# The lo half of every second weight part made by an adding DMA, in the output projection and gate of a bidirectional encoder layer

## The chip, the cores and the metric

The kernel runs on one core of a Trainium2 chip. The metric is the device time of one execution in microseconds; less is better. Profiles come from the hardware profiler, one execution each. Engines are named as in the profile: PE (matrix multiply; PEld loads its weights), DVE (vector engine), ACT (scalar engine), POOL (GpSimd), SP (the engine that issues most DMAs). Instructions that only issue a DMA are not counted as busy; an issuing queue is written with a q (SPq).

## The reference

One encoder layer over 256 tokens of width 2048, in float32:

```python
hn = _rmsnorm(h, norm_w[i])
proj = hn @ w_in[i]                                   # 2048 x 18432
q, v, f_fwd, f_bwd, z_a, b_gate, c_gate, h_b, z_b = jnp.split(proj, IN_SPLITS, axis=-1)
o_a = _hgrn2_bidirectional(jax.nn.silu(q), v, f_fwd, f_bwd, lb_all[:, i])
o_a = _head_rmsnorm(o_a, hgrn_norm_w[i]) * jax.nn.silu(z_a)
y_b = b_gate * _short_conv(c_gate * h_b, conv_w[i])
o_b = _rmsnorm(y_b, conv_norm_w[i]) * jax.nn.silu(z_b)
h = h + jnp.concatenate([o_a, o_b], axis=-1) @ w_out[i]   # 4096 x 2048
gate = jax.nn.sigmoid(h @ w_ple_gate[i])                  # 2048 x 2048
h = h + (p[i] @ w_ple[i]) * gate                          # 256 x 2048
return _rmsnorm(h, final_norm_w)
```

The change concerns the weights of the two products `@ w_out` and `@ w_ple_gate`.

## The kernel before

**Two halves for each number.** Each factor is kept as hi, the number cast to float32r, and lo, the number minus hi, also in float32r. A product is then hi x hi + hi x lo + lo x hi. In the output projection and the gate these are three matmuls, L636 (hi of the activations, hi of the weights), L637 (hi, lo) and L638 (lo, hi).

**The stream of weights.** All weights pass through the class `Stream`. `add` puts a block of the weights of up to 1 MB on the list `todo` and cuts it into parts of 128 x 1024 numbers (512 KB); a part has a number, its place in `where`. `load` issues the DMA of one block from SP's queue (L57) into a tile `raw` (3 buffers). `split` makes hi with a cast on ACT (L70) and lo with a subtraction on DVE (L71), in one tile `spl` (5 buffers) in which hi and lo rows alternate. `get(i)` returns part i and first opens all parts up to i + 3 (`ahead` is 3). Splits are emitted at a raised priority (`high_priority(offset=300)`). The order of the instructions on each engine comes from the tile framework's scheduler, by priority and readiness; only the first blocks of the kernel are ordered by hand.

**The stages.** (1) The input projection: 72 blocks of columns, `gemm_in`, L289 and L290, with the recurrence of group A and the convolution of group B worked in between. (2) The output projection: four blocks j of 512 columns, each with 8 blocks of 1 MB from `w_out`; `gemm_tok` runs over 32 row tiles, first those of group A into `pa`, then those of group B into `pb`, for both halves m of the tokens. A part of 128 x 1024 holds two row tiles of 512 columns, so PE runs 12 matmuls on it. After each j the residual `hh` is updated on DVE (L657, L661) and transposed for the next product (L646 on PE, L649 on ACT, L650 on DVE). (3) The gate: columns of 512, 512, 512, 256 and 256 (`GCOLS`); ahead of each 512 columns stands the product with `w_ple` (`pp`, one part, copied to `pl` in L722). In the two columns of 256 a part holds four row tiles. `gated` makes the sigmoid on ACT (L683), multiplies and adds on DVE (L686, L687), squares on ACT (L694) and multiplies by the final norm's weight on POOL (L695). The last column runs its four parts twice, first for m = 0, then for m = 1, each followed by `finish(m)`, which scales and stores.

At the border between (1) and (2) the last group of B is still being worked: POOL L314 and L587, ACT L580, L594 and L608, and the loads of `hh` (2 MB, L618) and `pr` (L622).

Of the kernel before, what the change touches and what calls it, by code (L numbers as in the profile page):

```python
# [11 lines left out]
AF = mybir.ActivationFunctionType  # L12
ALU = mybir.AluOpType
# [17 lines left out]
class Stream:  # L31


    def __init__(self, tc, rawp, splp, ahead):
        self.tc, self.nc, self.rawp, self.splp, self.ahead = tc, tc.nc, rawp, splp, ahead
        self.todo = []
        self.where = []
        self.raws = {}
        self.parts = {}
        self.next = 0  # L40

    def add(self, src):

        j = len(self.todo)
        _, k, n = src.shape
        self.todo.append((src, k, n))
        first = len(self.where)
        self.where += [(j, h) for h in range(k * n // 1024)]
        return list(range(first, len(self.where)))
# [9 lines left out]
    def open(self, i):  # L59
# [6 lines left out]
        self.parts[i] = part.rearrange("p (k s n) -> p k s n", s=2, n=n)  # L66
        return half, self.parts[i]

    def split(self, r, v):
        self.nc.scalar.copy(out=v[:, :, 0, :], in_=r)  # L70
        self.nc.vector.tensor_tensor(out=v[:, :, 1, :], in0=r, in1=v[:, :, 0, :], op=ALU.subtract)  # L71

    def get(self, i):
        while self.next <= min(i + self.ahead, len(self.where) - 1):
            if self.next not in self.parts:
                part = self.open(self.next)

                with self.tc.high_priority(offset=300):
                    self.split(*part)
            self.next += 1  # L80
        return self.parts[i]

# [2 lines left out]
def tile_hymba_encoder(  # L85
# [31 lines left out]
    ws = Stream(tc, rawp, splp, 3)  # L117
# [8 lines left out]
    oblocks = [sum((ws.add(w_out[j, h]) for h in range(8)), []) for j in range(4)]  # L126
    gblocks, pblocks = [], []
    for j, (c0, n) in enumerate(GCOLS):
        if c0 % 512 == 0:
            pblocks.append(ws.add(w_ple[c0 // 512]))  # L130
        if n == 512:
            gblocks.append(sum((ws.add(w_gate[j, h]) for h in range(4)), []))
        else:
            gblocks.append(sum((ws.add(w_gate_end[j - 3, h]) for h in range(2)), []))


    few = const.tile([P, 16], F32, name="few")
# [43 lines left out]
    for j in range(4):  # L181
        sgn = 1 if j < 2 else -1
        pool.affine_select(
            out=tri[:, j, :], in_=tri[:, j, :], compare_op=ALU.is_ge, fill=0.0, base=0,
# [369 lines left out]
    for i in range(8):  # L554
# [9 lines left out]
        for m in range(2):  # L564
            ct = 2 * i + m
            dve.tensor_scalar(cg[:, m, :], u[:, m, 0:T], cvw[:, 0, ct : ct + 1], None, op0=ALU.mult)
            for j in (1, 2):
                dve.scalar_tensor_tensor(
                    out=cg[:, m, :], in0=u[:, m, j : j + T], scalar=cvw[:, j, ct : ct + 1],
# [11 lines left out]
        for m in range(2):  # L581
            ct = 2 * i + m
            dve.scalar_tensor_tensor(
                out=hb[:, m, :], in0=hb[:, m, :], scalar=cnw[:, ct : ct + 1], in1=sz[:, m, :],
# [67 lines left out]
    for j in range(4):  # L652
# [7 lines left out]
        for m in range(2):  # L660
            dve.scalar_tensor_tensor(  # L661
                out=hh[:, m, cs], in0=pb[m], scalar=rb[:, m : m + 1], in1=hh[:, m, cs], op0=ALU.mult, op1=ALU.add
# [128 lines left out]
```

## Time and profile before

| | |
|---|---|
| runs | 1145.67, 1146.47, 1147.21 us; median 1146.47 |
| profiled execution, own time | 1148.26 us |
| its span in the profile | 1146.5 us |
| granted PE clock, mean | 0.994 |
| DMA, whole span | 214.31 MB, mean 187 GB/s |
| stage of the output projection and the gate | 860.65 to 1137.90 us of the span |

The profiled execution's own time is that of the execution that the profiler recorded; its span is the stretch from the first to the last instruction in it. In a line of a group, the columns are: line, engine and operation, tiles written and read, shapes, count, busy time and mean ns of one, and the idle time of the engine just before them with what ended it. In a timeline a line is start, duration, engine, line, operation; in brackets is the idle time before it and what ended it.

### The profile page before, as it was taken

Reading aid. Unit: us, or ns where it says so; the run is one execution under the profiler, and the core shown is the slowest. Engines: PE = TensorE matmul, PEld = TensorE weight load, DVE = VectorE, ACT = ScalarE, POOL = GpSimd, SP = SyncE. Lnnn points to the kernel's source line nnn. Section 1 sums busy time; section 2 is a strip of 40 time slices with the busy share of each in tenths; the row PEclk is TensorE's granted clock in tenths of the full one; section 3 lists DMA queues with packets and bytes.
Section 4 is the critical chain, followed back from the end, with each engine's and each line's share of the span. In section 5 each row is a group of like instructions: output and inputs, shape, how many; then the busy total and the mean of one; then the engine's idle time right before and its main releaser. Section 6 shows DMA issues by size and latency. Waiting matters only on the chain.

```text
span 1146.5 us, 16966 instructions
## 1 busy us (share of the span) xinstructions
PE 1130.4 (99%) x6832; PEld 980.6 (86%) x6832; DVE 739.8 (65%) x954; ACT 644.4 (56%) x896; POOL 210.9 (18%) x167
## 2 busy tenths in 40 slices
PE   8989999999999999999999999999999999999997
PEld 7878888888888888888888888888888888888886
DVE  7695859585858686775566566566656555555664
ACT  6676667585858585765544444444545434434554
POOL 1031414140413223232121211211211000000011
PEclk9999999999999999999999999999999999999999
DMA  9653545455455545464555555555557555565542
GB/s 317 261 196 111 189 156 190 165 182 177 156 185 177 170 169 184 152 214 153 188 197 198 185 184 188 187 198 182 201 184 266 187 198 192 194 216 188 202 166 75
DMA packets 32911, 214.31 MB, mean 187 GB/s; under 512 B 3648, under 2 KB 5056, under 8 KB 8512
## 3 DMA queue, kind: packets, MB, share of 16 engines
q1 hardware_dynamic: 32688, 213.14, 54.1%
q8 instruction: 54, 0.88, 0.3%
q14 instruction: 25, 0.20, 0.0%
q10 hardware_dynamic: 144, 0.08, 0.0%
HBM read 211.11 MB, written 2.10 MB: 186 GB/s over the span
## 4 chain that ended last, share of the span: by engine, by line
PE 97%; DMA 1%; ACT 1%; POOL 0%; DVE 0%; SPq 0%; issue 0%; ACTq 0%
PE a L289 46%; PE a L290 23%; PE pg L637 3%; PE pg L636 3%; PE pg L638 3%; PE pa L636 3%; PE pa L638 3%; PE pa L637 3%; PE pb L636 3%; PE pb L637 3%; PE pb L638 3%; PE scps L466 1%; PE cx L508 1%; PE o L518 1%; DMA xf<-in_xt_dram 1%; PE o L519 1%
## 5 line engine op out<-in xcount | busy, mean ns | idle before, releaser
L71 DVE TENSOR_TENSOR spl<-raw,spl 128x1024 fp32r<-128x1024 f32 (+2 forms) x394 | 503.7, 1281 | 324.9 <-ACT spl L70 324.4
L289 PE MATMUL a<-xs,spl 128*128 128x512 f32 x1792 | 632.0, 397 | 1.2 <-ACT spl L70 1.2
L70 ACT CAST spl<-raw 128x1024 fp32r<-128x1024 f32 (+2 forms) x394 | 406.6, 1035 | 354.9 <-PE a L290 219.3
L290 PE MATMUL a<-xs,spl 128*128 128x256 f32 x1792 | 501.5, 280 | 1.1 <-DVE spl L71 1.0
L289 PEld LDWEIGHTS a<-xs,spl 128*128 128x128 f32 x1792 | 337.4, 188 | 77.5 <-ACT spl L70 2.1
L290 PEld LDWEIGHTS a<-xs,spl 128*128 128x128 f32 x1792 | 338.9, 189 | 2.4 <-DVE spl L71 2.3
L289 PE MATMUL a<-spl,xs 128*128 128x512 f32 x512 | 178.6, 393 | 0.0
L290 PE MATMUL a<-spl,xs 128*128 128x256 f32 x512 | 143.6, 281 | 0.0
L289 PEld LDWEIGHTS a<-spl,xs 128*128 128x128 f32 x512 | 95.9, 187 | 21.4
L290 PEld LDWEIGHTS a<-spl,xs 128*128 128x128 f32 x512 | 96.9, 189 | 0.0
L309 ACT COPY r<-a 128x256 f32<-128x256 f32 x112 | 41.0, 368 | 45.1 <-PE a L290 45.0
L695 POOL TENSOR_TENSOR hh<-hh,fw 128x512 f32<-128x512 f32 (+1 forms) x10 | 11.5, 1152 | 259.2 <-ACT gt L694 249.7
L636 PE MATMUL pg<-spl,ht 128*128 128x512 f32 (+1 forms) x160 | 55.7, 348 | 0.0
L638 PE MATMUL pg<-spl,ht 128*128 128x512 f32 (+1 forms) x160 | 55.5, 347 | 0.0
L637 PE MATMUL pg<-spl,ht 128*128 128x512 f32 (+1 forms) x160 | 55.5, 347 | 0.0
L636 PE MATMUL pa<-spl,mixa 128*128 128x512 f32 x128 | 50.5, 394 | 0.0
L638 PE MATMUL pa<-spl,mixa 128*128 128x512 f32 x128 | 49.9, 390 | 0.0
L637 PE MATMUL pa<-spl,mixa 128*128 128x512 f32 x128 | 49.9, 390 | 0.0
L637 PE MATMUL pb<-spl,mixb 128*128 128x512 f32 x128 | 49.8, 389 | 0.0
L636 PE MATMUL pb<-spl,mixb 128*128 128x512 f32 x128 | 49.8, 389 | 0.0
L638 PE MATMUL pb<-spl,mixb 128*128 128x512 f32 x128 | 49.8, 389 | 0.0
L504 POOL TENSOR_TENSOR s<-scm 128x256 f32<-128x256 f32 x16 | 17.9, 1121 | 113.1 <-DVE scm L502 113.1
(166 smaller groups left out, 1093.5 us busy)
## 6 DMA issues: line engine op xcount, KB each, us to landing
raw<-in_w_in_dram SPq DMA_DIRECT2D x138, 1024.0 KB, 5.0
raw<-in_w_out_dram SPq DMA_DIRECT2D x32, 1024.0 KB, 5.0
raw<-in_w_gate_dram SPq DMA_DIRECT2D x12, 1024.0 KB, 5.0
raw<-in_w_in_dram SPq DMA_DIRECT2D x9, 512.0 KB, 10.2
raw<-in_w_gate_end_dram SPq DMA_DIRECT2D x4, 1024.0 KB, 4.9
xf<-in_xtok_dram SPq DMA_DIRECT2D x2, 1024.0 KB, 12.6
hh<-in_xtok_dram SPq DMA_DIRECT2D x1, 2048.0 KB, 7.9
raw<-in_w_ple_dram SPq DMA_DIRECT2D x4, 512.0 KB, 3.6
```

The lines of the kernel that those rows point to most:

```text
L70: self.nc.scalar.copy(out=v[:, :, 0, :], in_=r)
L71: self.nc.vector.tensor_tensor(out=v[:, :, 1, :], in0=r, in1=v[:, :, 0, :], op=ALU.subtract)
L289: pe.matmul(a, lhsT=lh, rhs=rf, start=(kt == 0), stop=False)
L290: pe.matmul(a[:, :T], lhsT=ll, rhs=rh, start=False, stop=(kt == NKT - 1))
L309: act.copy(out=r, in_=acc[m][:, 1, :])
L466: pe.matmul(scps[s0 : s0 + Q, 2 * d + hf, t0 : t0 + w], lhsT=lhsT, rhs=rhs, start=True, stop=True)
L504: pool.tensor_tensor(out=s, in0=sm[:, 0:2, :], in1=sm[:, 2:4, :], op=ALU.add)
L508: pe.matmul(cx[:, d, :], lhsT=kx[:, d, h, :], rhs=qc[:, d, h, :], start=True, stop=True)
L636: pe.matmul(acc[m], lhsT=lh, rhs=w[:, k, 0, :], start=(kt == 0), stop=False)
L637: pe.matmul(acc[m], lhsT=lh, rhs=w[:, k, 1, :], start=False, stop=False)
L638: pe.matmul(acc[m], lhsT=ll, rhs=w[:, k, 0, :], start=False, stop=(kt == nk - 1))
L695: pool.tensor_tensor(out=h, in0=h, in1=fw[:, cs], op=ALU.mult)
```

## The change

Every second part of the output projection's and the gate's weights (`late[1::2]`, 48 of 96 parts; always the second half of a block of 1 MB) is split in another way. ACT makes hi with the same cast as before and then writes -hi to the place of lo. A DMA issued from POOL's queue then reads the same 512 KB of weights from HBM once more and adds them to -hi in SBUF, so that lo stands there when it has landed. The DVE subtraction of these parts is gone. The product with `w_ple` and the whole input projection are split as before.

```diff
@@ class Stream
+        self.by_dma = ()
...
+    def split_by_dma(self, i, r, v):
+
+        j, h = self.where[i]
+        src, k, n = self.todo[j]
+        kp = 1024 // n
+        self.nc.scalar.copy(out=v[:, :, 0, :], in_=r)
+        self.nc.scalar.activation(v[:, :, 1, :], r, AF.Copy, scale=-1.0)
+        self.nc.gpsimd.dma_start(v[:, :, 1, :], src[:, kp * h : kp * h + kp], accum_op=ALU.add)
+
     def split(self, r, v):
...
                 with self.tc.high_priority(offset=300):
-                    self.split(*part)
+                    if self.next in self.by_dma:
+                        self.split_by_dma(self.next, *part)
+                    else:
+                        self.split(*part)
...
+    late = sum(oblocks, []) + sum((g for g in gblocks), [])
+    ws.by_dma = set(late[1::2])
```

## The prediction

> **What bounds the kernel now.** I read the page first (engine shares and the chain), then the busy time in the stage that the change touches, then the waits in it, and last the instructions of one part in order of time.
>
> ```profile
> span 1146.5 us, 16966 instructions
> PE 1130.4 (99%) x6832; PEld 980.6 (86%) x6832; DVE 739.8 (65%) x954; ACT 644.4 (56%) x896; POOL 210.9 (18%) x167
> PE 97%; DMA 1%; ACT 1%; POOL 0%; DVE 0%; SPq 0%; issue 0%; ACTq 0%
> ```
>
> PE is 99% busy and the chain of work that ended last is PE for 97% of the span. An average can hide a stage, so here is the stage of the output projection and the gate alone, from its first matmul to its last:
>
> ```profile
> core 0: us, PE busy (x) PEld busy (x) DVE busy (x) ACT busy (x) POOL busy (x), PEclk, DMA share, GB/s
> 860.65:1137.90 277.25, 277.21 (x1328) 233.39 (x1328) 153.41 (x155) 125.49 (x149) 14.34 (x11) 1.00 0.54 189
> ```
>
> PE is busy for 277.21 of 277.25 us at full granted clock. DVE, which loses work by the change, has 124 us to spare there. The waits in this stretch (engine, line, whom it waited for, total, times, longest) say who sets the pace:
>
> ```profile
> POOL hh L695 <- ACT gt L694: 249.7, 7, 195.6
> DVE spl L71 <- ACT spl L70: 117.1, 92, 1.7
> ACT spl L70 <- PE pb L638: 53.4, 32, 1.7
> ACT spl L70 <- PE pa L638: 42.5, 28, 1.7
> ACT spl L70 <- PE pg L638: 32.6, 20, 1.8
> ```
>
> No row has PE waiting. The splits wait for PE: ACT's cast of a part (hi, L70) waits until PE releases one of the five `spl` buffers. So faster splitting has nothing to give, and what matters is whether a split can become late.
>
> **The cover.** ACT in order of time, in the gate:
>
> ```profile
> 1052.31 1.05 ACT L70 CAST spl<-raw 128x1024 fp32r<-128x1024 f32 x1 [1.67 <-PE pg L638]
> 1055.03 1.05 ACT L70 CAST spl<-raw 128x1024 fp32r<-128x1024 f32 x1 [1.67 <-PE pg L638]
> ```
>
> One part takes PE 1055.03 - 1052.31 = 2.72 us. With five buffers the cast of part k starts when PE ends part k-5; PE then works on k-4 to k-1. The second half of a split therefore has 4 x 2.72 = 10.88 us from the start of the cast before PE asks for it. The wait of 1.67 us in front of each cast also shows that ACT has room for one more instruction of 1.05 us per pair of parts.
>
> **The change part by part.** The instructions of a split today (minimum/median/maximum in ns), in that stage:
>
> ```profile
> L70 ACT CAST spl<-raw x96: 1034/1050/1057, 859.9 to 1123.6; 128x1024 fp32r<-128x1024 f32 x96
> L71 DVE TENSOR_TENSOR spl<-raw,spl x96: 1216/1226/1636, 861.0 to 1124.6; 128x1024 fp32r<-128x1024 f32 x96
> L57 SPq DMA_DIRECT2D raw<-in_w_out_dram x27: 327/328/328, 865.9 to 1010.2; - x27
> ```
>
> Of 96 parts, `late[1::2]` takes 48, each time the second part of a 1 MB load. *Removed*: 48 x 1.226 = 59 us of DVE, off the path, worth nothing, since nothing waits for DVE there but the lo matmuls, which are covered. *Added on ACT*: an ACTIVATE with scale -1. The nearest rows are 128x512, the cast and the activations:
>
> ```profile
> L694 ACT ACTIVATE gt<-hh 128x512 f32<-128x512 f32 x6 | 3.8, 629 | 2.0 <-DVE hh L687 2.0
> L649 ACT CAST ht<-ht 128x512 fp32r<-128x512 f32 x8 | 4.7, 584 | 2.4 <-PE ht L646 2.4
> ```
>
> The two cost the same within 0.05 us, so at 128x1024 I take the cast's 1.05 us. It fits in the 1.67 us gap; -hi is there 2 x 1.05 = 2.10 us after the cast began. Four times, at the edges between gate columns, ACT is packed with L683, L694 and L722 and the extra 1.05 us pushes later casts: between 0 and 4.2 us in all, and I take 1.0, near the lower end, because gaps of 1.67 us follow each edge and give the time back.
>
> *Added on POOL*: the DMA is issued there and waits there for -hi. No POOL DMA is in this trace. Below is SP's 0.33 us (L57 above), above a POOL instruction on a tile:
>
> ```profile
> L587 POOL TENSOR_TENSOR cg<-cg,hb 128x512 f32<-128x512 f32 x1 | 2.3, 2292 | 3.6 <-DVE hb L583 3.6
> L314 POOL TENSOR_TENSOR hb<-hb,rbc 128x512 f32<-128x512 f32 x1 | 1.3, 1292 | 7.6 <-DVE hb L310 7.6
> ```
>
> I take 1.3 us. POOL is otherwise idle for almost 200 us on end, so nothing queues behind these waits in the output projection; L695 does in the gate, and nobody waits for L695 until the last lines.
>
> *Added on the DMA engines*: 48 x 0.5 MB, read a second time from HBM and added to what stands in SBUF. The trace has no adding DMA. Issues by line, with the time from issue to landing:
>
> ```profile
> raw<-in_w_ple_dram SPq DMA_DIRECT2D x4, 512.0 KB, 3.6
> raw<-in_w_out_dram SPq DMA_DIRECT2D x32, 1024.0 KB, 5.0
> hh<-in_xtok_dram SPq DMA_DIRECT2D x1, 2048.0 KB, 7.9
> xf<-in_xtok_dram SPq DMA_DIRECT2D x2, 1024.0 KB, 12.6
> DMA to landing us min/median/max: 4.8/5.0/9.6
> ```
>
> (The last line is for the raw loads from 866 to 960 us.) The lower end is a plain 512 KB, 3.6 us. The upper end is 12.6 us, a load in the saturated start. In between: the raw buffer's last reader is now the -1 activation, so SP issues the next 1 MB load just when the adding DMA starts, and both use the same engines; if the sum counts twice (source and destination are read), 2 MB are on their way together, and 2 MB took 7.9 us. That is the row it is nearest to, and I take 7.9.
>
> So lo lands 2.10 + 1.3 + 7.9 = 11.3 us after the cast began (6.0 at the lower end, 2.10 + 2.3 + 12.6 = 17.0 at the upper), against a cover of 10.88: late by 0.4 us. Between the cast of part k and its use lie two other parts of the new kind, whose waits also give time; with a wait w in front of each, 3w = 11.3 - 10.88, so w = 0.14 us, on 46 parts (all but the last two) 6.4 us. At the upper end w = 2.04 us, 94 us in all; at the lower end nothing.
>
> Two places have less cover. At the start (part 0 is the stage's first):
>
> ```profile
> 870.48 1.05 ACT L70 CAST spl<-raw 128x1024 fp32r<-128x1024 f32 x1
> 879.64 0.39 PE L636 MATMUL pa<-spl,mixa 128*128 128x512 f32 x1
> ```
>
> This is the cast of part 7, late behind L594, and the first matmul that uses it: 9.16 us. In that stretch the `hh` load of 2 MB is in flight and raw loads took up to 9.6 us, so lo lands 2.10 + 1.3 + 9.6 = 13.0 us after the cast: 3.8 us of waiting once (0 if it lands in 5.0). At the end:
>
> ```profile
> 1117.00:1126.00 9.00, 9.00 (x77) 9.00 (x77) 5.26 (x5) 3.82 (x5) 1.45 (x1) 1.00 0.01 3
> 1123.56 1.05 ACT L70 CAST spl<-raw 128x1024 fp32r<-128x1024 f32 x1 [1.84 <-PE pg L638]
> 1125.94 0.28 PE L637 MATMUL pg<-spl,ht 128*128 128x256 f32 x1
> 1126.06 0.28 PE L638 MATMUL pg<-spl,ht 128*128 128x256 f32 x1
> ```
>
> The last part is cast at 1123.56. The last column begins at about 1126.1 and reads four parts for one half of the tokens, 12 matmuls of 0.12 us each, so the fourth is needed at 1126.1 + 36 x 0.12 = 1130.4: a cover of 6.8 us. The DMA engines are empty there (share 0.01 in the first row), so I take 5.0 us, 512 KB counted twice: 2.10 + 1.3 + 5.0 = 8.4, 1.6 us late.
>
> The sum: 6.4 + 3.8 + 1.6 + 1.0 = 12.8 us. The profiled execution took 1148.26 us for its span of 1146.5, so it would take 1161.1; it lies 1.8 us above the median of the runs, 1146.47, to which the same 12.8 us give 1159.3 us.
>
> The Trainium skill, "DMA: Bandwidth & Descriptors", section "Anatomy of one DMA — SWDGE (gpsimd) path", fits a DMA from this queue at 2.0 us and bytes over 436 GB/s; by that a part lands in an estimated 3.2 us, lo is there 2.1 + 3.2 = 5.3 us after the cast, and the sum would be nothing. No run here shows that path, and the raw loads' 5.0 us against 4.4 by the same fit say that it is on the low side when the engines are half busy.
>
> **The rivals.**
>
> *The DMA engines become the bound.* A period of two parts now:
>
> ```profile
> 920.00:925.44 5.44, 5.44 (x25) 4.50 (x25) 2.45 (x3) 2.10 (x2) 0.00 (x0) 1.00 0.59 200
> 878.00:883.00 5.00, 5.00 (x23) 4.14 (x23) 3.33 (x4) 2.19 (x4) 0.00 (x0) 1.00 1.02 424
> ```
>
> One load of 1 MB fills 0.59 of 5.44 us. If the adding DMA costs as much, the share is 1.18 and a pair takes 6.42 us, 0.98 more; 46 x 0.98 + 1.6 at the end = 46.7 us, 1193 us. For it: the share. Against it: full engines moved 424 GB/s (second row), and 2 MB per 5.44 us are 385. The Trainium skill, "Collectives: The Full Stack", section "The bandwidth ceiling: the fold count and why AG ≠ RS ≠ AR", says that an add in the DMA runs at half a copy's rate since it reads two sources through one ring; by that rule the doubled cost holds and this rival's sum stands. No run so far shows an add.
>
> *The add itself is slow*, by many short descriptors (rows of 2 KB and 1 KB instead of 8 KB) or at its issue: 11.3 us become 17.0, 94 + 3.8 + 1.6 = 99 us, 1246 us. Against it: no row of the trace is that slow outside the saturated start.
>
> *The issue stands behind another POOL instruction.*
>
> ```profile
> 1063.19 1.05 ACT L70 CAST spl<-raw 128x1024 fp32r<-128x1024 f32 x1
> 1065.48 1.38 POOL L695 TENSOR_TENSOR hh<-hh,fw 128x512 f32<-128x512 f32 x1 [195.56 <-ACT gt L694]
> 1068.97 1.45 POOL L695 TENSOR_TENSOR hh<-hh,fw 128x512 f32<-128x512 f32 x1 [2.11 <-ACT gt L694]
> ```
>
> A part cast at 1063.19 has its -hi at 1065.3; behind both L695 its DMA starts only at 1070.4, 5.1 us later. On top of 0.4 that is 5.5 us at each of four column ends, 22 us with the 12.8: 1181 us. Against it: the splits are given priority in the order.
>
> *All hidden* (the other side, no change): if lo is there at most 6.8 + 2.3 = 9.1 us after its cast, only the last column is late, by no more than 2.3 us: 1146.5 us. It decides at an add that lands within 9.1 - 2.1 - 1.3 = 5.7 us. For it: a 512 KB load lands in 3.6, a 1 MB load in 5.0.
>
> *Faster* would need a wait of PE that DVE causes; the waits show none.
>
> **How the numbers follow.** The three runs lie 1.5 us apart, and 0.2% is 2.3 us, about what a measurement of this kernel can tell from no change. Chances: a little late, as summed, 0.30; DMA engines the bound 0.20; slow add 0.12; POOL's order 0.10; all hidden 0.23; faster by something not seen 0.05. So slower 0.72, within 0.2% 0.23, faster 0.05. The range goes from the hidden case, 1145.5 us with half of the runs' spread, to the slow add, 1246 us, and leaves out about 0.15; the likeliest case's own range is 1149 to 1170 us.
>
> **What would show it.** Right: PE in the changed trace waits in front of the lo matmuls L637 (their new lines) for a DMA, some 0.1 to 0.5 us per second part, more at part 7 and in the last column; ACT has 48 activations of about 1.05 us; landing of the adding DMA near 8 us beside a load and near 5 us in the last column; DMA share near 0.85 to 1.1. Wrong: no wait of PE in the stage (all hidden), a landing above 10 us (slow add), a share at 1 with the raw loads late as well (the engines), or waits only at the ends of the gate's columns (POOL's order).

## The result, and the profile after

The kernel before takes 1146.84 us and the changed kernel 1202.67 us (medians of four runs each). The ratio is 1.0474, with a 95% interval of 1.0458 to 1.0490: slower by some 55 us, 43 us above the forecast of 1159.3. That lies inside the whole range (to 1246 us) and outside the likeliest case's own (1149 to 1170 us). (One of the four runs after, 1216.96 us at a lower clock, is left out of the ratio.) The profiled execution took 1197.82 us, its span is 1196.1.

The page of the changed kernel, engine shares and chain:

```profile
span 1196.1 us, 17162 instructions
PE 1143.7 (96%) x6832; PEld 984.8 (82%) x6832; DVE 684.0 (57%) x906; ACT 689.2 (58%) x944; POOL 268.8 (22%) x215
PE 83%; DMA 12%; issue 2%; ACT 1%; POOL 0%; DVE 0%; SPq 0%; POOLq 0%; ACTq 0%
```

PE has as many matmuls as before, DVE 48 instructions fewer, ACT and POOL 48 more. DMA, 1% of the chain before, now makes 12% of it. The stage of the output projection and the gate, and PE's waits in it (total, times, longest):

```profile
858.50:1187.50 329.00, 293.31 (x1331) 240.04 (x1330) 99.44 (x110) 168.74 (x195) 69.99 (x58) 0.96 0.91 235
PE pa L654 <- DMA spl<-in_w_out_dram: 14.7, 6, 5.3
PE pb L654 <- DMA spl<-in_w_out_dram: 10.9, 5, 4.5
PE pg L654 <- DMA spl<-in_w_gate_dram: 8.9, 5, 3.6
PE pg L654 <- DMA spl<-in_w_gate_end_dram: 1.2, 1, 1.2
```

The stage takes 329.0 us instead of 277.25. Of the 51.8 us, 35.7 are these waits, all at L654, the matmul with the lo of the weights (L637 before), all for an adding DMA. The other 16.1 are PE itself, busy for 293.31 instead of 277.21 us with the same matmuls at a granted clock of 0.96. Where those come from is seen behind a long wait, PE in order of time:

```profile
885.22 0.80 PE L654 MATMUL pa<-spl,mixa 128*128 128x512 f32 x1 [5.34 <-DMA spl<-in_w_out_dram]
885.81 0.63 PE L655 MATMUL pa<-spl,mixa 128*128 128x512 f32 x1
886.24 0.63 PE L653 MATMUL pa<-spl,mixa 128*128 128x512 f32 x1
...
889.17 0.40 PE L654 MATMUL pa<-spl,mixa 128*128 128x512 f32 x1
889.41 0.39 PE L655 MATMUL pa<-spl,mixa 128*128 128x512 f32 x1
```

Behind the wait of 5.34 us the matmuls start 0.43 us apart, from 889.2 on 0.24: for four microseconds PE runs at about half its pace, with the granted clock at 0.59 from 885 to 890 us.

The new instructions, and the DMAs from issue to landing:

```profile
L76 ACT ACTIVATE spl<-raw x48: 1049/1056/1057, 850.7 to 1172.7; 128x1024 fp32r<-128x1024 f32 x48
L77 POOL DMA_DIRECT2D spl<-in_w_out_dram x32 | 38.6, 1205 | 164.7 <-ACT spl L76 158.1
raw<-in_w_out_dram SPq DMA_DIRECT2D x32, 1024.0 KB, 7.8
spl<-in_w_out_dram POOLq DMA_DIRECT2D x32, 512.0 KB, 10.2
spl<-in_w_gate_end_dram POOLq DMA_DIRECT2D x4, 512.0 KB, 6.1
q0 software_dynamic: 14080, 25.17, 12.0%
```

The activation takes 1.06 us and the issue 1.2 us. The adds land after 10.2 us, and the loads beside them after 7.8 instead of 5.0. The last line is the adds' queue: packets, MB, and their share of the 16 engines over the span. One add holds all engines for 0.12 x 1196.1 / 48 = 2.99 us.

One late add, from the cast of its part to the matmul that waits for it (the third line has the landing of the add issued at 925.60):

```profile
923.29 1.05 ACT L75 CAST spl<-raw 128x1024 fp32r<-128x1024 f32 x1 [1.62 <-PE pa L655]
925.60 1.20 POOL L77 DMA_DIRECT2D spl<-in_w_out_dram  x1 [5.70 <-ACT spl L76]
spl<-in_w_out_dram POOLq DMA_DIRECT2D x1, 512.0 KB, 13.2
938.87 0.79 PE L654 MATMUL pa<-spl,mixa 128*128 128x512 f32 x1 [4.50 <-DMA spl<-in_w_out_dram]
```

925.60 + 13.2 = 938.8 is the moment at which PE goes on. So the landing counts from the start of the issue, and the 1.2 us of the issue lie in it. The issue starts 2.3 us after the cast, and lo is there 2.3 + 13.2 = 15.5 us after it. Against the cover of 10.88 us that is 4.6 late; PE waits 4.50.

### The profile page after: what moved, and what is told of

The parts are those of the page before. It is cut to its first block, busy times and chain, and to the rows that moved or that the text cites. A ratio compares the mean times of both kernels' runs of the same rounds, so it can differ in the third digit from the quotient of the medians.

```text
span 1196.1 us, 17162 instructions
## 1 busy us (share of the span) xinstructions
PE 1143.7 (96%) x6832; PEld 984.8 (82%) x6832; DVE 684.0 (57%) x906; ACT 689.2 (58%) x944; POOL 268.8 (22%) x215
## 4 chain that ended last, share of the span: by engine, by line
PE 83%; DMA 12%; issue 2%; ACT 1%; POOL 0%; DVE 0%; SPq 0%; POOLq 0%; ACTq 0%
PE a L306 44%; PE a L307 22%; DMA spl<-in_w_out_dram 8%; DMA spl<-in_w_gate_dram 3%; PE pa L654 2%; PE pg L654 1%; PE pb L654 1%; PE pa L655 1%; PE pg L655 1%; PE pb L655 1%; PE pa L653 1%; PE pg L653 1%; PE pb L653 1%; PE scps L483 1%; PE cx L525 1%
## 5 line engine op out<-in xcount | busy, mean ns | idle before, releaser
L81 DVE TENSOR_TENSOR spl<-raw,spl 128x1024 fp32r<-128x1024 f32 (+2 forms) x346 | 444.4, 1288 | 358.8 <-ACT spl L80 358.5
L80 ACT CAST spl<-raw 128x1024 fp32r<-128x1024 f32 (+2 forms) x346 | 356.2, 1032 | 278.7 <-PE a L307 212.4
L75 ACT CAST spl<-raw 128x1024 fp32r<-128x1024 f32 x48 | 50.4, 1050 | 66.2 <-PE pb L655 27.8
L77 POOL DMA_DIRECT2D spl<-in_w_out_dram x32 | 38.6, 1205 | 164.7 <-ACT spl L76 158.1
L654 PE MATMUL pa<-spl,mixa 128*128 128x512 f32 x128 | 52.8, 413 | 14.7 <-DMA spl<-in_w_out_dram 14.7
L654 PE MATMUL pg<-spl,ht 128*128 128x512 f32 (+1 forms) x160 | 56.7, 355 | 10.0 <-DMA spl<-in_w_gate_dram 8.9
L654 PE MATMUL pb<-spl,mixb 128*128 128x512 f32 x128 | 51.8, 405 | 10.9 <-DMA spl<-in_w_out_dram 10.9
L653 PE MATMUL pg<-spl,ht 128*128 128x512 f32 (+1 forms) x160 | 56.3, 352 | 0.0
L655 PE MATMUL pg<-spl,ht 128*128 128x512 f32 (+1 forms) x160 | 56.3, 352 | 0.0
L653 PE MATMUL pa<-spl,mixa 128*128 128x512 f32 x128 | 52.3, 409 | 0.0
L655 PE MATMUL pa<-spl,mixa 128*128 128x512 f32 x128 | 52.1, 407 | 0.0
L655 PE MATMUL pb<-spl,mixb 128*128 128x512 f32 x128 | 51.2, 400 | 0.0
L653 PE MATMUL pb<-spl,mixb 128*128 128x512 f32 x128 | 51.1, 400 | 0.0
## 6 DMA issues: line engine op xcount, KB each, us to landing
spl<-in_w_out_dram POOLq DMA_DIRECT2D x32, 512.0 KB, 10.2
xf<-in_xtok_dram SPq DMA_DIRECT2D x2, 1024.0 KB, 13.2
```

The lines of the kernel that those rows point to most:

```text
L77: self.nc.gpsimd.dma_start(v[:, :, 1, :], src[:, kp * h : kp * h + kp], accum_op=ALU.add)
L653: pe.matmul(acc[m], lhsT=lh, rhs=w[:, k, 0, :], start=(kt == 0), stop=False)
L654: pe.matmul(acc[m], lhsT=lh, rhs=w[:, k, 1, :], start=False, stop=False)
L655: pe.matmul(acc[m], lhsT=ll, rhs=w[:, k, 0, :], start=False, stop=(kt == nk - 1))
```

## The experiments

Two theories. *Lateness*: lo lands 2.3 + 10.2 = 12.5 us after its cast, later than the cover of 10.88 us; more cover, or an earlier landing, cures it. (Some expectations below say 2.1 + 1.2 + 10.2 = 13.5 us: they count the issue a second time.) *Full engines*: an add costs the DMA engines so much that they, not PE, set the pace; only less DMA work cures it. Rivals to both were the second read of HBM as such, the short rows, and ACT's and POOL's part.

**Is it the DMA at all?**

```diff
-        self.nc.gpsimd.dma_start(v[:, :, 1, :], src[:, kp * h : kp * h + kp], accum_op=ALU.add)
```

> The adding DMA is left out (lo stays -hi); ACT's second instruction and the missing DVE subtraction stay. Both theories: no wait of PE, 1146 to 1149 us. If the second activation on ACT or the changed order costs something, it shows here alone: over 1149 us.

1146.66 us, ratio 1.0003 (0.9993 to 1.0012). ACT's activation, the missing subtraction and the order cost nothing that these runs can tell.

**A copy in place of the add.**

```diff
-... src[:, kp * h : kp * h + kp], accum_op=ALU.add)
+... src[:, kp * h : kp * h + kp])
```

> The DMA of the new parts copies the weights into the place of lo and adds nothing (so lo is the weight itself, the sum with -hi is left out); queue, bytes, rows and order stay. Engines full because an add costs about twice a copy (in the changed kernel's trace 3.2 us of full DMA engines per 1 MB load and 2.95 per 512 KB add, 6.2 us per pair of parts against PE's 5.44): a copy costs half, 3.2 + 1.5 = 4.7 us, the share falls to about 0.85 and the time to 1147 to 1155 us. Second read of HBM as such, or POOL's queue and its short rows: nothing changes, 1190 to 1205 us.

1153.02 us, ratio 1.0057 (1.0040 to 1.0074). Its DMA lines:

```profile
raw<-in_w_out_dram SPq DMA_DIRECT2D x32, 1024.0 KB, 5.0
spl<-in_w_out_dram POOLq DMA_DIRECT2D x32, 512.0 KB, 6.1
q0 software_dynamic: 14080, 25.17, 7.0%
L77 POOL DMA_DIRECT2D spl<-in_w_out_dram x32 | 23.1, 722 | 148.1 <-ACT spl L76 133.9
```

The same packets and bytes hold the engines for 0.07 x 1153.2 / 48 = 1.68 us and land after 6.1. Reading the weights twice is thus almost free; adding them is not. An add costs the engines 2.99 / 1.68 = 1.8 times a copy, and its issue takes 1.2 us instead of 0.72. The landing of 6.1 us is what changes the wait: 2.3 + 6.1 = 8.4 us is well inside the cover. What is left of the loss is one wait of 3.5 us at the start, beside the 2 MB load of `hh`, and the slower pace behind it.

**More cover.** A sixth buffer of split weights from the output projection on.

```diff
+        pool, tag = (self.more, "spm") if self.more is not None and i % 6 == 5 else (self.splp, "spl")
+        part = pool.tile([P, 2048], F32R, tag=tag, name=f"spl{i}")
...
+    ws.more = ctx.enter_context(tc.tile_pool(name="more", bufs=1, side="left", reuse_waits="tile"))
+    ws.ahead = 4
```

> A sixth buffer of split weights from the output projection on, and parts opened four ahead: the cover grows from 4 to 5 parts, 10.88 to 13.6 us. Landing too late for the cover (2.1 + 1.2 + 10.2 = 13.5 us after the cast): almost all of the loss goes, 1147 to 1155 us. Engines full: 48 pairs at 6.17 instead of 5.44 us remain, 35 us, 1180 to 1195 us.

1168.74 us, ratio 1.0203 (1.0173 to 1.0234): below the range of full engines, far above that of lateness. Neither theory alone fits. Busy times from 880 to 1110 us, first of the changed kernel, then with the sixth buffer (the last three columns are granted clock, DMA share and GB/s):

```profile
880.00:1110.00 230.00, 202.27 (x847) 163.02 (x848) 62.27 (x62) 111.36 (x118) 41.00 (x34) 0.94 0.93 244
880.00:1110.00 230.00, 223.24 (x993) 182.50 (x992) 74.32 (x75) 132.84 (x145) 52.02 (x43) 1.00 1.02 272
```

With more cover PE does 993 instead of 847 matmuls in the same time, at full clock, and only now are the engines wholly full (1.02). In the changed kernel they were not (0.93): a split waits for PE to release a buffer, so a wait of PE also holds back the next loads. The adds still land after 10.2 us in the median, and 2.3 + 10.2 = 12.5 us fits the new cover of 13.6. What is left are 15.2 us of waits in nine places, 6.5 of them at the start, for adds that landed after 11.5 us or more.

**Fewer adds.** First every fourth part with five buffers, then with six and none in the first ten parts.

```diff
-    ws.by_dma = set(late[1::2])
+    ws.by_dma = set(late[3::4])
```

> Only every fourth part gets the adding DMA (24 instead of 48). Engines full: four parts need 2 x 3.2 + 2.95 = 9.4 us of 10.88, so the engines keep up, landing falls to 6 to 8 us and the time to 1147 to 1157 us. Landing too late by itself: the same landing near 10 us and half of the loss, 1170 to 1178 us.

1165.12 us, ratio 1.0169 (1.0149 to 1.0189), against both ranges. The engines have room here (0.81), yet some adds come too late:

```profile
880.00:1110.00 230.00, 222.73 (x978) 182.33 (x979) 99.40 (x93) 113.56 (x125) 28.38 (x23) 0.99 0.81 230
spl<-in_w_out_dram POOLq DMA_DIRECT2D x16, 512.0 KB, 8.4
```

The median add is in time, 2.3 + 8.4 = 10.7 us. PE waits 12.3 us in eight places: 4.8 at the start, 1.2 in the last column, and between them for single adds that landed late. The one issued at 931.88 landed after 10.2 us, which is 2.3 + 10.2 - 10.88 = 1.6 us late, and PE waits 1.5.

> Six buffers of split weights (cover 13.6 us) and an add in every fourth part only, none of them in the first ten parts of the output projection. Late landing against the cover: 2.1 + 1.2 + 8.4 = 11.7 us after the cast fits, nothing is late, 1146 to 1149 us. If an add costs something else as well (the path of POOL, the engines): 10 us or more remain, over 1155 us.

1147.92 us, ratio 1.0018 (1.0005 to 1.0031), with landing at 8.3 us and no wait of PE in the trace. 2.3 + 8.3 = 10.6 us under a cover of 13.6 cost nearly nothing.

**Which loads does an add meet?** The first part of each 1 MB load instead of the second; the next load is issued when the second part is split, so the add no longer starts together with it.

```diff
-    ws.by_dma = set(late[1::2])
+    ws.by_dma = set(late[0::2])
```

> The first part of each 1 MB load takes the adding DMA instead of the second, so that the add is issued some 3 us ahead of the next load and not together with it. Engines nearly full in any case (3.05 + 3.0 us of each 5.44): landing stays near 10 us, 1190 to 1208 us. Add and load starting together is what makes the add late: landing 7 to 8 us as in the run that adds from SBUF, 1165 to 1175 us.

1166.03 us, ratio 1.0166 (1.0147 to 1.0185).

```profile
spl<-in_w_out_dram POOLq DMA_DIRECT2D x32, 512.0 KB, 8.0
880.00:1110.00 230.00, 217.71 (x944) 176.31 (x944) 71.52 (x73) 126.75 (x137) 47.37 (x39) 0.98 1.00 270
```

As many adds, the same queue and cover, and the landing falls from 10.2 to 8.0 us, while the engines stay full (1.00). Starting together with a load is thus what made the adds of the second part land so late. PE still waits 14.4 us, 4.9 of them at the start.

**The source.** From the raw tile in SBUF, with a fourth raw buffer, and the control with the buffer alone.

```diff
-... src[:, kp * h : kp * h + kp], accum_op=ALU.add)
+... r, accum_op=ALU.add)
```

> The add reads the weights from the raw tile in SBUF instead of from HBM a second time (a fourth raw buffer covers the later release). Two reads in the DMA engines wherever they come from: landing and share stay, 1185 to 1205 us. HBM's reading as the limit: the share falls, landing goes to 6 to 8 us, 1147 to 1165 us.

> The changed kernel with a fourth raw buffer, as in the run that adds from SBUF, but adding from HBM. If the fourth buffer was what helped there: 1165 to 1175 us. If it was the source in SBUF or the later release of the raw tile: as the changed kernel, 1192 to 1206 us.

From SBUF 1171.81 us, ratio 1.0203 (1.0176 to 1.0231), landing at 7.3 us; the control 1199.63 us, ratio 1.0452 (1.0427 to 1.0477). The buffer is not what helps. The engines' time per add stays:

```profile
spl<-raw POOLq DMA_DIRECT2D x48, 512.0 KB, 7.3
q0 software_dynamic: 14080, 25.17, 12.4%
```

0.124 x 1172.6 / 48 = 3.03 us, so HBM is not what makes an add long. Here too the next load waits until the add has landed, so the two start together less often; whether the source by itself gives anything stays open.

**Rows and size.** In the tiles of the new parts hi ahead of lo, so that a row is 4 KB; and half of the rows only.

```diff
+        if i in self.by_dma:
+            self.parts[i] = part.rearrange("p (s k n) -> p k s n", s=2, n=n)
```

> In the tiles of the new parts all of hi stands ahead of all of lo, so that the adding DMA moves one row of 4 KB per partition instead of two of 2 KB (or four of 1 KB); bytes and order stay. If the add is late because its short rows are many, or take turns with the loads' 8 KB rows: landing falls from 10.2 to 7 or 8 us and the time to 1160 to 1175 us. If the engine's time goes by bytes read (twice those of a copy): landing stays near 10 us, 1192 to 1205 us.

```diff
+        kq = kp // 2
+        self.nc.gpsimd.dma_start(v[:, :kq, 1, :], src[:, kp * h : kp * h + kq], accum_op=ALU.add)
```

> Each adding DMA adds only the first half of its rows (256 KB; the other half of lo stays -hi), five buffers as in the changed kernel. Landing set by the engines' time per add (3.0 us of all engines for 512 KB, so 1.5 for half; 3.05 + 1.5 = 4.55 us of each pair's 5.44, like the plain copy): landing 6 to 7 us, 1147 to 1157 us. A fixed price of an add from this queue, whatever its size: landing over 9 us, over 1175 us.

Long rows: 1188.09 us, ratio 1.0365 (1.0346 to 1.0383), between the two ranges. The adds still land after 10.2 us, but hold the engines for 0.111 x 1187.1 / 48 = 2.75 us. Short rows are a part of it, some 12 of the 54 us. Half the size: 1157.43 us, ratio 1.0089 (1.0074 to 1.0104).

```profile
spl<-in_w_out_dram POOLq DMA_DIRECT2D x32, 256.0 KB, 7.9
q0 software_dynamic: 7424, 12.59, 6.3%
```

The engines' time halves (0.063 x 1156.5 / 48 = 1.52 us), so there is hardly a fixed price in it; the landing falls by only 2.3 us, less than I expected. The load that starts with the add is still there, which may be why; this was not tried.

**The start.**

```diff
-    ws.by_dma = set(late[1::2])
+    ws.by_dma = set(late[9::2])
```

> The first four adding DMAs, which run beside the 2 MB load of the residual, are made in the old way (44 adds instead of 48). If the start has a loss of its own (the trace shows 5.3 us of waiting there and half the clock for some 4 us after it): 7 to 10 us less than the changed kernel, 1192 to 1196 us. If all adds cost the same: 44/48 of the loss, 1198 us.

1197.00 us, ratio 1.0440 (1.0399 to 1.0482), not separable from the changed kernel; the four runs lie between 1190.8 and 1203.6 us, too far apart to decide. In the trace the first long wait only comes later, 4.18 us at 888.4 instead of 5.34 at 885.2.

**The clock.** The kernel before, with repeated casts that hold five parts back; no adding DMA.

```diff
+        for _ in range(1 + again):
+            self.nc.scalar.copy(out=v[:, :, 0, :], in_=r)
...
+    ws.again = {late[18]: 10, late[34]: 12, late[52]: 14, late[72]: 11, late[80]: 13}
```

> The kernel before, without any adding DMA; in five parts of the late stage ACT makes the same cast 11 to 15 times over, so that PE has to wait once each, about 1.9, 3.0, 4.0, 5.1 and 6.1 us. If a wait of over some 3 us by itself halves the granted clock afterwards: matmuls of 0.43 us behind the longer waits, 1.7 to 2 us extra each, in all 20 us of waits and 5 to 8 us more, 1172 us. If full DMA engines slow PE: the matmuls keep 0.227 us, 1166 us.

1193.3 us in one run. The waits came out longer than planned, up to 9.9 us, since the casts behind were held back too. Two of PE's instructions, and the stretch behind the wait:

```profile
912.70 1.22 PE L641 MATMUL pa<-spl,mixa 128*128 128x512 f32 x2 [4.08 <-ACT spl L72]
914.97 0.63 PE L642 MATMUL pa<-spl,mixa 128*128 128x512 f32 x1
913.00:916.00 3.00, 2.96 (x7) 1.86 (x7) 0.90 (x1) 0.00 (x0) 0.00 (x0) 0.50 0.36 66
```

The granted clock is 0.50 with the DMA engines at 0.36: the wait halves the clock, not the DMA. The Trainium skill, "TensorE: Matmul & The Clock Gate", section "Why this matters for your kernels", asks for no gap of PE over about 3 us for this reason. The trace agrees for the waits shown, of 4 and 5 us. Shorter waits are mixed; in the trace of the changed kernel:

```profile
965.20 0.50 PE L654 MATMUL pb<-spl,mixb 128*128 128x512 f32 x1 [2.02 <-DMA spl<-in_w_out_dram]
966.71 0.39 PE L654 MATMUL pb<-spl,mixb 128*128 128x512 f32 x1
1051.77 0.50 PE L654 MATMUL pb<-spl,mixb 128*128 128x512 f32 x1 [1.81 <-DMA spl<-in_w_out_dram]
1053.54 0.63 PE L654 MATMUL pb<-spl,mixb 128*128 128x512 f32 x1
```

Behind 2.02 us of waiting a matmul keeps its 0.39 us; behind 1.81 us it takes 0.63 from some 1.3 us later on. So a wait under 3 us can cost the clock too, and these traces give no sharp limit.

**Both cures, and with less work.** Six buffers and the first part of each load; then the same with a copy in place of the add.

> Both cures of the lateness at once: six buffers, and the add in the first part of each load. If the engines' time is a bound of its own (share 1.0 in the two runs with one cure, 6.05 us of engine time per pair where PE needs 5.75 with what lies between the parts; 48 x 0.3 = 14 us): 1158 to 1168 us, share 0.98 to 1.0, no better than the better of the two by more than 8 us. If only lateness costs: 1146 to 1152 us.

> The same with a plain copy in place of the add (lo is the weight itself, the sum with -hi is left out). The engines need 3.05 + 1.63 = 4.7 us per pair: nothing waits, 1146 to 1150 us, share 0.83. If the second read or POOL's queue costs PE something on its own: as the adding one.

1159.46 us, ratio 1.0113 (1.0087 to 1.0140), and 1146.64 us, ratio 1.0006 (0.9996 to 1.0015). From 880 to 1110 us, first with the add, then with the copy:

```profile
880.00:1110.00 230.00, 223.61 (x988) 183.14 (x988) 75.48 (x74) 131.87 (x145) 51.30 (x42) 0.99 1.01 276
880.00:1110.00 230.00, 230.00 (x1032) 190.46 (x1031) 78.57 (x78) 137.19 (x151) 33.96 (x44) 1.00 0.90 294
```

With the add PE waits 9.7 us in six places: 5.2 us in all before 892 us, beside the load of `hh`; 2.2 us at 1032.9, for an add issued 0.4 us before the 1 MB load of `fw`, the final norm's weight; and 2.3 us at 1092.6. Between the first two groups there is no wait (the same run):

```profile
895.00:1030.00 135.00, 135.00 (x607) 111.53 (x606) 42.80 (x43) 76.54 (x79) 28.88 (x24) 1.00 1.04 283
```

So full engines alone do not slow PE in this stretch; the waits stand mostly where yet another load joins. With the copy no wait is left. So the loss has two parts. 1.0474 - 1.0113, some 41 us, goes with the two cures of lateness, clock included. 1.0113 - 1.0006, some 12 us, goes only with a cheaper DMA. The copy holds the engines for less time and lands earlier as well (5.6 instead of 9.2 us); which of the two it is was not separated. No version beats the kernel before; the best ones equal it, as PE bounds it.

## Why the prediction was right and wrong

*Right*: that PE bounds the stage, that the removed subtraction is worth nothing, the cover of 10.88 us (a late add's wait came out of it, 4.6 against 4.50 us), and the 1.05 us on ACT (1.06). The wait in the last column, forecast at 1.6 us, is 1.2. That the loss shows as waits of the lo matmul for the adding DMA was right as well, and so was the DMA share of 0.85 to 1.1 (0.91).

*The step that failed* is the landing, "and I take 7.9". It is 10.2. The row chosen, one load of 2 MB, was a single stream; here an add and a load start together on engines that have hardly a pause. Set apart from the load, as many adds land after 8.0. The other terms of the sum come out as follows: the waits between start and end at 27.8 instead of 6.4 us, the start at 6.7 instead of 3.8, the last column at 1.2 instead of 1.6, the edges of the gate's columns on ACT at nothing that can be told instead of 1.0.

*Luck*: the sum adds 1.3 us for the issue to the landing, which has the issue in it. The size is right (1.2), the addition is not. Without it the chosen landing gives 2.1 + 7.9 = 10.0 us, inside the cover, and between start and end there would have been no wait to forecast. With what was measured, 2.3 + 10.2 = 12.5, the formula gives w = (12.5 - 10.88) / 3 = 0.54 us and on 46 parts 25 us, near the 27.8 of the trace. The mechanism held and its main term was mis-sized.

*What was missing* is the clock. The forecast spread the waits evenly, 0.14 us each. They came bunched, up to 5.3 us in 17 places, and the longer ones cost PE its clock: most of the 16.1 us. The trace shows how a bunch ends. The adds issued at 925.6, 931.0 and 936.5 landed after 13.2, 13.7 and 12.3 us. PE waited 4.50 us for the first and not for the other two, which had by then got its time as well. From 944 to 950 us the engines were down to a share of 0.30, and the next add, at 949.0, landed after 8.0. What sets the length of this cycle was not tried.

*At the start* the wait for part 7 was forecast at 3.8 us from a landing of 9.6; the trace has 5.3 and a landing of 13.3, and 1.4 us more for part 5. Leaving those adds out gained nothing that the runs can tell.

*The rivals.* The engines as the bound, with 1193 us, came nearest to the time, and the doubled cost of an add that it rested on is there, 1.8 times a copy by the engines' time. The Trainium skill, "Collectives: The Full Stack", section "The bandwidth ceiling: the fold count and why AG ≠ RS ≠ AR", has half a copy's rate for the add of a ReduceScatter, because it reads two sources. Measured are 1.8 here. This rival's signs, a share at 1 and late raw loads, came in part: 0.91, and 7.8 instead of 5.0 us. But what is left when both cures of lateness are in is 12 us, not 46, and at a share of 1.04 PE ran for 135 us without a wait. That the time is near is thus no support for its mechanism.

The slow add had as its sign a landing above 10 us, and 10.2 just meets it. Its price, 99 us, did not come, and its reasons are small parts here: long rows give back some 12 us and leave the landing at 10.2, and the issue takes 1.2 us. POOL's order was not it: the waits stand in the output projection too, where no L712 is in the queue. All hidden was put at a landing of 5.7 us, or 7.0 without the issue counted twice; a lone add in the last column meets that with some 6, the adds beside loads do not.

*The fit* of the Trainium skill, "DMA: Bandwidth & Descriptors", section "Anatomy of one DMA — SWDGE (gpsimd) path", 3.2 us for 512 KB by estimate, was too low for this use: the plain copy lands after 6.1 us and the add after 10.2.

## What to carry to other kernels

Before work is moved to a DMA, ask whether its landing beside the loads that start with it, not its landing alone, fits into the time from the last producer to the first use; that time is set by the number of buffers. See from which moment a landing is counted before adding the issue to it. Where an engine is 99% busy, relief of another engine is worth nothing, and every microsecond that it has to wait is paid in full, and often more than in full, since the clock of PE fell behind the long waits and some short ones. An adding DMA is no free addition: here it cost the DMA engines 1.8 times a copy.

## What was unexpected of the hardware

An add of 512 KB into SBUF holds the 16 DMA engines for 2.99 us against 1.68 for a copy of the same bytes and rows, and 3.03 us when both operands lie in SBUF; its issue on POOL takes 1.2 us against 0.72. With half as many adds the engines' time per add is the same, 0.063 x 1162.1 / 24 = 3.05 us. Counted from the start of the issue it lands after 6.0 us alone, after 10.2 when it starts together with a 1 MB load, and after 8.0 when it starts some 3 us ahead of one. Behind a wait of PE of 4 to 5 us the matmuls ran at 0.43 us instead of 0.23 for some two to five microseconds, with the DMA engines at a share of 1.05 and of 0.36. Behind waits of about 2 us this happened in some places and not in others.
